# Layer 2 of a two-layer block: where the merge logits and retention gates are projected

## The chip, the cores and the metric

The kernel runs on one core of one Trainium2 chip. Its time is device microseconds of one execution, from the first to the last instruction; lower is better. All arithmetic is 32-bit: the matmuls take float32 values split into two fp32r parts (a rounded one and the rest), three products for each.

## The reference, cut to what matters

The program computes two transformer-like layers for 1,024 tokens of width 1,024. The change lies in the second layer alone:

```python
h = rms_norm(x, norm_gain[layer])
proj = jnp.einsum('bsd,dc->bsc', h, w_in[layer])          # 10 x 1024 columns
(sb_q, sb_k, sb_v, sb_g, r_q, r_k, r_v, r_g, m_sb, m_ret) = jnp.split(proj, SPLIT_POINTS, axis=-1)
...
out_a = merge_heads(stick_breaking_attention(qa, ka, va)) * jax.nn.silu(sb_g)   # 8 heads of 128
...
out_b = merge_heads(ret) * jax.nn.silu(r_g)               # chunkwise retention, 4 heads of 256
p_a = jnp.einsum('bsw,wd->bsd', out_a, w_branch_sb[layer])
p_b = jnp.einsum('bsw,wd->bsd', out_b, w_branch_ret[layer])
merged = (jax.nn.sigmoid(m_sb + b_merge[layer, 0]) * p_a
          + jax.nn.sigmoid(m_ret + b_merge[layer, 1]) * p_b)
x = x + jnp.einsum('bsd,de->bse', merged, w_out[layer])
```

The merge logits are `m_sb` and `m_ret` (columns 8192 to 10239 of the projection, 16 blocks of 128) and the retention gates are `r_g` (columns 7168 to 8191, 8 blocks of 128). Both depend only on `h`, and both are first read in the last part, where the two branches are gated and merged.

## The kernel before, in words

The normalized input of layer 2, `h2T`, stays in SBUF with the model dimension on partitions, in two parts (`h2h`, `h2l`). Every projection is a stream of matmuls over 8 slices of the model dimension and 3 products. `dense_tok` (L92) makes token-major results, 24 matmuls for each 128 tokens; `dense_col` (L107) makes a block of 128 columns for all 1,024 tokens, 48 matmuls of 512 columns into two PSUM banks; `dense_half` (L116) makes one half of such a block, 24 matmuls into one bank. These accumulators share 3 PSUM banks (tag "a").

Weights come through `load_units` (L74): for each of the 8 slices a DMA into one of 3 `raw` buffers (L64), then the split into two fp32r parts, as a rule on GpSimd (L70 a copy that rounds, L71 the difference), for the stick-breaking heads half on ScalarE and VectorE (L67, L68). The split units, `wu`, have 10 buffers of 512 columns.

Layer 2 then has these stages, in program order:

1. Eight stick-breaking heads (L970). Each has a projection of q, k and v (192 matmuls of 384 columns, L102), a per-token norm and a transposition on VectorE (L132), the head's gate (48 matmuls of 512 columns, L112), and then a chain for each of three blocks: scores (L1025), a scan on VectorE (L1039) with steps on ScalarE and GpSimd around it, transposes on TensorE (L1055), and products with v (L1060).
2. `merge_logits(0)`, 4 of the 16 blocks of merge logits, each half block evicted by ScalarE (L956) and stored by a DMA.
3. Four retention heads (L1189), each `ret_proj(h)` and then `ret_chain(h)`. `ret_proj` loads 8 units for q and k (512 columns) and projects them (192 matmuls, L112), rotates them on VectorE and GpSimd (L1100 to L1105) in place in the tiles `ro` (3 buffers for q and 3 for k, two used by a head), loads 8 units that hold v and the gate together (256 columns each), projects v (192 matmuls of 256 columns, L102), and then the gate (two blocks, 96 matmuls, L112). `ret_chain` goes through 8 chunks of 128 tokens in two groups of 4: scores of a group (L1132), transposed and decayed k (`kf`, `kd`, L1142 to L1144), and for each chunk the products L1152 and L1160, an output norm, the state's update (L1171 and VectorE) and its split (L1181, L1182). The tiles `kf` and `ob` (the transposed output) share one buffer.
4. `merge_logits(1)` to `(3)`, the other 12 blocks.
5. `gated` (L1200) loads the two branches' outputs and gates, multiplies and splits them; between and after it come the two branch projections and the output projection. Its tiles take space that the retention stage must have given back.

The order on each engine is not that of the program text: a list scheduler of the framework moves an instruction ahead when its inputs and buffers are there in the scheduler's own plan, and prefers what stands earlier in the program. On the chip the order on each engine is then fixed, and a late input holds what stands behind it. So the projection of head h+1 is already spread between the chain steps of head h.

Of the kernel before, what the change touches and what calls it, by code (L numbers as in the profile page):

```python
# [11 lines left out]
F32 = mybir.dt.float32  # L12
# [15 lines left out]
def f32(ap):  # L28
    return ap.bitcast(F32)
# [7 lines left out]
def tile_kernel(ctx: ExitStack, tc: tile.TileContext, I: dict, out: bass.AP, dbg=None, stop=None):  # L37
# [22 lines left out]
    # ---------------------------------------------------------------- helpers  # L60
# [67 lines left out]
    def dve_transpose(dst, src):  # L128
        """dst[c, x, r, t] = src[t, x, r, c], 128 by 128 for every x and r, in blocks of 32 by 32"""
        for a in range(4):  # L130
            for b in range(4):
                nc.vector.transpose(out=dst[32 * b:32 * b + 32, :, :, 32 * a:32 * a + 32],  # L132
                                    in_=src[32 * a:32 * a + 32, :, :, 32 * b:32 * b + 32])
# [54 lines left out]
    # DRAM scratch  # L188
# [14 lines left out]
    # ---------------------------------------------------------------- layer 1: norm  # L203
# [28 lines left out]
    # constants  # L232
# [7 lines left out]
    # ---------------------------------------------------------------- layer 1: dz + gates  # L240
# [25 lines left out]
    # gate scalars, [token in chunk, dir*4+head, chunk]  # L266
# [32 lines left out]
    # ---------------------------------------------------------------- layer 1: delta heads  # L299
# [4 lines left out]
    for h in range(4):  # L304
# [20 lines left out]
        # q: raw, with its norm per token  # L325
# [8 lines left out]
        # k: token major, normalized, and back  # L334
# [32 lines left out]
        for d in range(2):  # L367
# [13 lines left out]
            # decay [s, c]: with its diagonal for the products with q, strictly above it for the system  # L381
            # (the backward system is stored transposed)
# [41 lines left out]
        # operands of the scan  # L424
# [23 lines left out]
    # ---------------------------------------------------------------- layer 1: inverses of the 64-blocks  # L448
# [28 lines left out]
    # ---------------------------------------------------------------- layer 1: neighbourhood attention  # L477

    def na_proj(p, hold):
# [13 lines left out]
        for m, acc in dense_tok(hT, us, 0, 384):  # L493
            j = m % 4
            sq = na1.tile([P, 256], F32, tag="sq", name="sq", bufs=2)
            nc.scalar.activation(out=sq, in_=acc[:, 0:256], func=AF.Square)
            ss = na1.tile([P, 4], F32, tag="ss", name="ss", bufs=2)
            nc.vector.tensor_reduce(out=ss, in_=sq.rearrange("p (h d) -> p h d", h=4), op=ALU.add, axis=AX.X)
            rsqrt_small(ss, ss, 1.0 / 64, EPS, 4)
            kn = na1.tile([P, P], F32, tag="kn", name="kn", bufs=5)  # L500
            nc.scalar.copy(out=qn[:, m, :], in_=acc[:, 0:128])
            nc.scalar.copy(out=kn, in_=acc[:, 128:256])
            nc.scalar.copy(out=v[:, m, :], in_=acc[:, 256:384])
            for x, t_ in enumerate((qn[:, m, :], kn)):
                t_ = t_.rearrange("p (h d) -> p h d", h=2)
                nc.vector.tensor_tensor(out=t_, in0=t_, in1=ss[:, 2 * x:2 * x + 2].unsqueeze(2).to_broadcast([P, 2, 64]),
                                        op=ALU.mult)
            kns.append(kn)
            if j == 3:
                sl = slice((m - 3) * P, (m + 1) * P)  # L510
                # head 0 keeps its rounded part above the rest, head 1 the other way round
                pt = bank("a")
                for jj, k_ in enumerate(kns):
                    nc.tensor.transpose(pt[:, jj * P:(jj + 1) * P], k_, ident)
                for hh in range(2):
                    a, b = slice(hh * 64, hh * 64 + 64), slice(64 - hh * 64, 128 - hh * 64)
                    nc.scalar.activation(out=kS[hh][a, sl], in_=pt[a, :], func=AF.Copy, scale=gk[a])
                    nc.vector.scalar_tensor_tensor(out=kS[hh][b, sl], in0=pt[a, :], scalar=gk[a],  # L518
                                                   in1=f32(kS[hh][a, sl]), op0=ALU.mult, op1=ALU.subtract)
                kns = []  # L520
            yield 1
# [4 lines left out]
    def na_attn(p, tiles):  # L526
        qn, kS, v, z, TB = tiles[p]

        def scores(t, hh, st):
# [24 lines left out]
            if rl != ru:  # L554
                # the second row's window starts one row later: its last row takes the place of the first
                nc.tensor.matmul(ps[64:128, 0:64], lhsT=q2[:, hh, :], rhs=f32(kS[hh][:, (rl + 8) * 64:(rl + 9) * 64]),
                                 start=True, stop=True)
# [93 lines left out]
    # ---------------------------------------------------------------- layer 1: delta rule scan  # L651
# [193 lines left out]
    # ---------------------------------------------------------------- layer 1: output (transposed), layer 2: norm  # L845
    # the tokens in two sets: the inner 512, which the scan leaves first, and the outer 512
# [93 lines left out]
    # ---------------------------------------------------------------- layer 2: stick breaking attention  # L940
# [10 lines left out]
    def merge_logits(q):  # L951
        us = load_units(I["w_in_2"], 8192 + 512 * q, 512)
        for b in range(4):
            for half, acc in enumerate(dense_col(h2T, us, b * P)):
                lg = mp.tile([P, 512], F32, tag="lg", name="lg", bufs=2)
                nc.scalar.activation(out=lg, in_=acc, func=AF.Identity, bias=bm[:, 4 * q + b:4 * q + b + 1])  # L956
                nc.sync.dma_start(out=d_sg[4 * q + b, :, half * 512:half * 512 + 512], in_=lg)
# [7 lines left out]
    with tc.tile_pool(name="sb", bufs=1) as sb, tc.tile_pool(name="sr", bufs=1, side="right") as sr:  # L965
# [4 lines left out]
        for h in range(8):  # L970
# [43 lines left out]
            for ib in (0,1):  # L1014
                po = bank("o")
                ini = sb.tile([P, 4], F32, tag="ini", name="ini", bufs=2)
                for diag in ((True, False) if ib else (True,)):
                    c0 = ib * 512 if diag else 0
                    As = []
                    for i4 in range(4):  # L1020
# [28 lines left out]
                        As.append(A)  # L1049
                    for kb in range(4):  # L1050
# [14 lines left out]
                nc.sync.dma_start(out=d_oa[h, :, ib * 512:ib * 512 + 512], in_=ov)  # L1065
    if "oa" in dbg:
        nc.sync.dma_start(out=dbg["oa"], in_=d_oa)
# [3 lines left out]
    merge_logits(0)  # L1071

    # ---------------------------------------------------------------- layer 2: retention
    d_ob = dram.tile([8, P, T], F32, name="d_ob")
    d_gb = dram.tile([8, P, T], F32, name="d_gb")
    with tc.tile_pool(name="rt", bufs=1) as rt:
# [11 lines left out]
        def ret_proj(h):  # L1088
# [18 lines left out]
            us = load_units(I["w_in_2"], 6144 + 256 * h, 256, parts=2, stride=1024)  # L1107
# [7 lines left out]
            for b in range(2):  # L1115
                for half, acc in enumerate(dense_col(h2T, us, 256 + b * P)):
                    gv = mp.tile([P, 512], F32, tag="lg", name="gv", bufs=2)
                    nc.scalar.copy(out=gv, in_=acc)
                    nc.sync.dma_start(out=d_gb[2 * h + b, :, half * 512:half * 512 + 512], in_=gv)
            return rot[0], rot[1], vs  # L1120

        def ret_chain(h, tiles):
            qTs, kTs, vs = tiles
            state = None
            for g in range(2):
                qT, kT, v = qTs[g], kTs[g], vs[g]
                # scores^T of four chunks
# [19 lines left out]
                for j in range(4):  # L1147
# [6 lines left out]
                    if n > 0:  # L1154
# [3 lines left out]
                        for b in range(2):  # L1158
                            for x, (a, c) in enumerate(PASSES):
                                nc.tensor.matmul(po[:, :256], lhsT=qs[a][:, b, :], rhs=ss_[c][:, b, :], start=False,  # L1160
                                                 stop=(b == 1 and x == 2))
                    ss = rt.tile([P, 1], F32, tag="ss", name="ss", bufs=2)
# [28 lines left out]
    for q in range(1, 4):  # L1191
        merge_logits(q)
# [3 lines left out]
    # ---------------------------------------------------------------- layer 2: branches and merge  # L1196
# [135 lines left out]
```

## Time and profile before

| | |
|---|---|
| median of 3 runs | 2333.45 us (2331.77 to 2336.94) |
| the profiled execution's own time (span) | 2331.9 us |
| TensorE matmul busy | 2182.4 us (94%), 12,069 matmuls |
| VectorE busy | 1414.8 us (61%) |
| GpSimd busy | 1252.0 us (54%) |
| ScalarE busy | 863.7 us (37%) |
| mean granted TensorE clock | 0.98 |

Times of the trace count from the start of the span. The stick-breaking heads take about 830 to 1450 us, the retention heads 1450 to 1980 us, and the gating and the branch and output projections the rest. A matmul's busy time in the profile reaches from its issue to a modelled end, and consecutive matmuls overlap, so the busy share overstates how full TensorE is; the distance between consecutive matmuls in an undisturbed stream is the better measure of what one costs.

### The profile page before, as it was taken

The page shows a single profiled execution, that of the slowest core. Times are in us where ns is not written, and L with a number is a line of the kernel's source. Part 1 is how long each engine was busy: PE and PEld are TensorE (multiplying, and loading weights), DVE is VectorE, ACT ScalarE, POOL GpSimd, SP SyncE. Part 2 cuts the span into 40 slices and gives each one's busy share as a digit, 9 for nine tenths or more (in the row PEclk, how much of TensorE's full clock was granted, in tenths as well). Part 3 has the DMA queues.
Part 4 walks back from the last instruction along what each step waited for, and adds up shares of the span by engine and source line. Part 5 has one row for each costly group of instructions (what it writes and reads, how often), then busy time and mean ns, then how long its engine had stood idle before and what let it go on. Part 6 is the DMA issues. An engine that isn't in the chain of part 4 may idle for free.

```text
span 2331.9 us, 33715 instructions
## 1 busy us (share of the span) xinstructions
PE 2182.4 (94%) x12069; PEld 1864.4 (80%) x12069; DVE 1414.8 (61%) x2596; ACT 863.7 (37%) x2126; POOL 1252.0 (54%) x1467
## 2 busy tenths in 40 slices
PE   7998888999999999899889999999999999989999
PEld 7776877787888798787788777788888888767887
DVE  4688789844456568887877784426474744343221
ACT  5344334445554235554555544112222222332210
POOL 6667778851004256565565664536363633666531
PEclk9999999999999999999999999999999999999999
DMA  4266820154475421111011112211111122666433
GB/s 131 80 170 166 203 80 26 37 165 132 154 279 205 153 84 46 50 55 55 10 50 50 55 50 72 72 56 46 64 46 64 46 82 91 226 213 211 140 109 108
DMA packets 236488, 240.86 MB, mean 103 GB/s; under 512 B 39776, under 2 KB 173600, under 8 KB 236064
## 3 DMA queue, kind: packets, MB, share of 16 engines
q1 hardware_dynamic: 236320, 238.71, 32.5%
q8 instruction: 95, 1.56, 0.3%
q14 instruction: 73, 0.60, 0.1%
HBM read 167.31 MB, written 71.34 MB: 102 GB/s over the span
## 4 chain that ended last, share of the span: by engine, by line
PE 33%; DVE 16%; POOL 7%; issue 4%; DMA 4%; ACT 4%; SPq 0%; POOLq 0%; ACTq 0%; DVEq 0%
PE acc L112 21%; PE acc L102 5%; DVE qf L132 4%; PE acc L859 3%; DVE A L1039 3%; POOL A L1044 2%; DMA raw<-in_w_in_dram 1%; POOL wu L71 1%; DVE A L1035 1%; POOL ss L126 1%; DMA oa<-d_oa 1%; DVE ob L132 1%; DVE sq L988 1%; DVE wT L1058 1%; PE pt L1160 1%
## 5 line engine op out<-in xcount | busy, mean ns | idle before, releaser
L112 PE MATMUL acc<-h2h,wu 128*128 128x512 f32 x1504 | 459.1, 396 | 6.7 <-DVE sq L988 2.7
L102 PE MATMUL acc<-wu,h2h 128*128 128x384 f32 (+1 forms) x1536 | 376.2, 327 | 13.4 <-DVE sq L988 4.2
L71 POOL TENSOR_TENSOR wu<-raw,wu 128x512 fp32r<-128x512 f32 (+3 forms) x268 | 363.4, 1365 | 6.3
L70 POOL TENSOR_SCALAR wu<-raw 128x512 fp32r<-128x512 f32 (+3 forms) x268 | 205.9, 772 | 250.7 <-PE acc L112 176.7
L112 PEld LDWEIGHTS acc<-h2h,wu 128*128 128x128 f32 x1504 | 281.5, 188 | 71.9 <-ACT lg L956 3.1
L102 PEld LDWEIGHTS acc<-wu,h2h 128*128 128x128 f32 x1536 | 272.2, 194 | 21.5 <-issue 3.5
L112 PE MATMUL acc<-h2l,wu 128*128 128x512 f32 x752 | 276.1, 396 | 0.0
L102 PE MATMUL acc<-wu,h2l 128*128 128x384 f32 (+1 forms) x768 | 250.1, 327 | 0.0
L102 PE MATMUL acc<-wu,h1hi 128*128 128x384 f32 (+2 forms) x768 | 193.1, 335 | 12.6 <-DVE kS L518 6.7
L112 PE MATMUL acc<-h1hi,wu 128*128 128x512 f32 x512 | 164.3, 409 | 8.0 <-ACT pad L315 4.7
L112 PEld LDWEIGHTS acc<-h2l,wu 128*128 128x128 f32 x752 | 141.4, 188 | 31.0
L102 PEld LDWEIGHTS acc<-wu,h1hi 128*128 128x128 f32 x768 | 138.5, 196 | 17.0 <-issue 8.0
L1044 POOL TENSOR_TENSOR A<-Z,A 128x128 f32<-128x128 f32 (+2 forms) x96 | 112.4, 1176 | 70.5 <-DVE A L1039 43.6
L102 PEld LDWEIGHTS acc<-wu,h2l 128*128 128x128 f32 x768 | 148.4, 193 | 1.0
L102 PE MATMUL acc<-wu,h1lo 128*128 128x384 f32 (+2 forms) x384 | 127.8, 335 | 0.0
L112 PEld LDWEIGHTS acc<-h1hi,wu 128*128 128x128 f32 x512 | 98.1, 193 | 33.0 <-ACT pad L315 6.2
L126 POOL TENSOR_TENSOR ss<-ss,mhalf 128x2 f32<-128x2 f32 (+2 forms) x136 | 115.6, 851 | 7.2
L132 DVE STREAM_TRANSPOSE qf<-sq 32x256 f32<-32x256 f32 x256 | 111.6, 436 | 4.0
L125 POOL TENSOR_SCALAR ss<-ss 128x2 f32<-128x2 f32 (+2 forms) x136 | 42.5, 312 | 117.7 <-ACT sq L982 47.0
L1060 PE MATMUL po<-wT,v 128*128 128x512 f32 (+3 forms) x288 | 76.1, 365 | 22.2 <-DVE wT L1058 12.2
L112 PE MATMUL acc<-h1lo,wu 128*128 128x512 f32 x256 | 96.4, 405 | 0.0
L112 PE MATMUL acc<-oah,wu 128*128 128x512 f32 x256 | 81.3, 413 | 10.0 <-DVE sg L1232 6.1
(547 smaller groups left out, 4770.5 us busy)
## 6 DMA issues: line engine op xcount, KB each, us to landing
raw<-in_w_in_dram SPq DMA_DIRECT2D x192, 256.0 KB, 2.8
d_pk<-sct SPq DMA_DIRECT2D x24, 512.0 KB, 4.3
raw<-in_w_out_dram SPq DMA_DIRECT2D x40, 256.0 KB, 2.8
wsa<-d_pk SPq DMA_DIRECT2D x16, 512.0 KB, 6.0
wsb<-d_pk SPq DMA_DIRECT2D x16, 512.0 KB, 7.1
d_sg<-lg SPq DMA_DIRECT2D x32, 256.0 KB, 2.6
sg<-d_sg SPq DMA_DIRECT2D x32, 256.0 KB, 4.3
raw<-in_w_in_dram SPq DMA_DIRECT2D x32, 192.0 KB, 2.7
```

What stands on the lines that cost most here:

```text
L70: nc.gpsimd.tensor_scalar(out=u[:, 0, :], in0=raw, scalar1=1.0, scalar2=0.0, op0=ALU.mult, op1=ALU.add)
L71: nc.gpsimd.tensor_tensor(out=u[:, 1, :], in0=raw, in1=f32(u[:, 0, :]), op=ALU.subtract)
L102: nc.tensor.matmul(acc[:, :n], lhsT=hT[a][:, k, m * P:(m + 1) * P], rhs=us[k][:, b, c0:c0 + n], start=(k == 0 and i == 0), stop=(k == NK - ...
L112: nc.tensor.matmul(accs[half], lhsT=us[k][:, b, c0:c0 + P], rhs=hT[a][:, k, half * 512:(half + 1) * 512], start=(k == 0 and i == 0), stop= ...
L125: nc.gpsimd.tensor_scalar(out=dst, in0=src, scalar1=mul, scalar2=eps, op0=ALU.mult, op1=ALU.add)
L126: nc.gpsimd.tensor_tensor(out=dst, in0=dst, in1=mhalf[:, :eshape], op=ALU.pow)
L132: nc.vector.transpose(out=dst[32 * b:32 * b + 32, :, :, 32 * a:32 * a + 32], in_=src[32 * a:32 * a + 32, :, :, 32 * b:32 * b + 32])
L859: nc.tensor.matmul(acc, lhsT=us[k][:, y, (b % 4) * P:(b % 4 + 1) * P], rhs=token_set(mT[x][:, k, 0:T], s), start=(k == 0 and i == 0), stop ...
L988: nc.vector.scalar_tensor_tensor(out=sq[:, a * P:(a + 1) * P], in0=acc[:, a * P:(a + 1) * P], scalar=ss[:, a:a + 1], in1=gqk[:, a, :], op0 ...
L1039: nc.vector.tensor_tensor_scan(out=A[:, :w][:, ::-1], data0=A[:, :w][:, ::-1], data1=A[:, :w][:, ::-1], initial=0.0 if diag else ini[:, i4 ...
L1044: nc.gpsimd.tensor_tensor(out=A[:, :w], in0=Z[:, :w], in1=A[:, :w], op=ALU.subtract)
L1060: nc.tensor.matmul(po[:, i0 * P:512], lhsT=v[a][:, c0 // P + kb, :], rhs=wT[b][:, :n], start=(diag and kb == 0 and x == 0), stop=(diag == ...
```

## The change

The function `merge_logits` and its calls are gone. In its place a generator, `filler`, goes through 24 blocks of 128 columns, the 16 of the merge logits first and then the 8 of the retention gates. For each block it loads two units of 4 slices each into buffers of its own (`fu`, 3 of them, beside the 10 of `wu`; `raw` and the accumulators are shared as before), splits them on GpSimd, and gives the two halves one after the other with `dense_half`, each with its eviction and its store. The program takes half blocks from it in these places: one in each of the three blocks of every stick-breaking head, between the scan steps and the transposes (24), five after the last of these heads, and one in each of the 8 chunks of the last retention head's chain, between the output's products and its norm. What is left (11) follows that chain. `ret_proj` loads and projects v alone, without the gate.

```diff
-    def merge_logits(q):
-        us = load_units(I["w_in_2"], 8192 + 512 * q, 512)
-        for b in range(4):
-            for half, acc in enumerate(dense_col(h2T, us, b * P)):
+    d_gb = dram.tile([8, P, T], F32, name="d_gb")
+    fp = ctx.enter_context(tc.tile_pool(name="fp", bufs=1))
+
+    def filler(blocks):
+        for b in blocks:
+            cols = slice(8192 + b * P, 8192 + (b + 1) * P) if b < 16 else slice(7168 + (b - 16) * P, 7168 + (b - 15) * P)
+            us = []
+            for g in range(2):
+                raw = wraw.tile([P, 4, P], F32, tag="raw", name="raw", bufs=3)
+                nc.sync.dma_start(out=raw, in_=I["w_in_2"][g * 512:(g + 1) * 512, cols].rearrange("(k p) c -> p k c", p=P))
+                u = fp.tile([P, 2, 4, P], F32R, tag="fu", name="fu", bufs=3)
+                nc.gpsimd.tensor_scalar(out=u[:, 0], in0=raw, scalar1=1.0, scalar2=0.0, op0=ALU.mult, op1=ALU.add)
+                nc.gpsimd.tensor_tensor(out=u[:, 1], in0=raw, in1=f32(u[:, 0]), op=ALU.subtract)
+                us += [u[:, :, k, :] for k in range(4)]
+            for half in range(2):
+                hs = slice(half * 512, half * 512 + 512)
+                acc = dense_half(h2T, us, 0, half)
                 lg = mp.tile([P, 512], F32, tag="lg", name="lg", bufs=2)
...
+                if b < 16:
+                    nc.scalar.activation(out=lg, in_=acc, func=AF.Identity, bias=bm[:, b:b + 1])
+                    nc.sync.dma_start(out=d_sg[b, :, hs], in_=lg)
+                else:
+                    nc.scalar.copy(out=lg, in_=acc)
+                    nc.sync.dma_start(out=d_gb[b - 16, :, hs], in_=lg)
+                yield 1
+
+    fill = filler(range(24))
...
                         last_sb = nc.scalar.activation(out=A[:, :w], in_=A[:, :w], func=AF.Exp)
                         As.append(A)
+                    take(fill, 1)
                     for kb in range(4):
...
+        take(fill, 5)
...
-    merge_logits(0)
...
-            us = load_units(I["w_in_2"], 6144 + 256 * h, 256, parts=2, stride=1024)
+            us = load_units(I["w_in_2"], 6144 + 256 * h, 256)
...
-            for b in range(2):
-                for half, acc in enumerate(dense_col(h2T, us, 256 + b * P)):
-                    gv = mp.tile([P, 512], F32, tag="lg", name="gv", bufs=2)
-                    nc.scalar.copy(out=gv, in_=acc)
-                    nc.sync.dma_start(out=d_gb[2 * h + b, :, half * 512:half * 512 + 512], in_=gv)
...
+                    if h == 3:
+                        take(fill, 1)
                     ss = rt.tile([P, 1], F32, tag="ss", name="ss", bufs=2)
...
-    for q in range(1, 4):
-        merge_logits(q)
+    drain(fill)
```

## Rows read from the trace of the kernel before

**Rows 1.** The page, part 1: busy time of each engine over the span.

```profile
PE 2182.4 (94%) x12069; PEld 1864.4 (80%) x12069; DVE 1414.8 (61%) x2596; ACT 863.7 (37%) x2126; POOL 1252.0 (54%) x1467
```

**Rows 2.** Busy time by stretch: window, its length, busy us (and count) by engine.

```profile
1002.00:1374.00 372.00, 333.16 (x1758) 293.38 (x1757) 298.52 (x580) 189.07 (x561) 219.59 (x286) 0.99 0.14 43
1374.00:1450.00 76.00, 74.74 (x358) 60.96 (x357) 46.30 (x77) 34.98 (x80) 43.35 (x55) 1.00 0.20 67
1865.00:1980.00 115.00, 115.00 (x559) 95.75 (x558) 55.30 (x103) 27.72 (x56) 45.25 (x54) 1.00 0.26 85
1980.00:2120.00 140.00, 125.00 (x511) 96.35 (x510) 61.13 (x65) 48.24 (x78) 93.53 (x76) 0.98 0.67 221
```

**Rows 3.** The chain of waits in order of time: start us, us, engine and line.

```profile
854.31 16.62 PE acc L102 x93
...
1451.11 23.25 PE acc L112 x100
...
1622.79 6.65 PE acc L102 x56
```

**Rows 4.** TensorE's waits, 1076 to 1374 us: total us, times, longest.

```profile
PE po L1060 <- DVE wT L1058: 7.6, 10, 1.8
PE po L1060 <- ACT wT L1057: 4.5, 4, 2.3
```

**Rows 5.** Instructions on tile `raw`, 1000 to 1460 us: count, ns min/median/max.

```profile
L64 SPq DMA_DIRECT2D raw<-in_w_in_dram x55: 327/374/642, 1013.3 to 1459.7; - x55
L70 POOL TENSOR_SCALAR wu<-raw x36: 614/624/1066, 1011.3 to 1457.0; 128x512 fp32r<-128x512 f32 x36
L71 POOL TENSOR_TENSOR wu<-raw,wu x36: 1265/1292/1731, 1012.0 to 1457.7; 128x512 fp32r<-128x512 f32 x36
...
L68 DVE TENSOR_TENSOR wu<-raw,wu x19: 691/1249/1772, 1019.0 to 1317.5; 128x512 fp32r<-128x512 f32 x19
...
DMA to landing us min/median/max: 2.6/2.9/5.1
```

**Rows 6.** Line 956, whole span: the eviction of one half block of merge logits.

```profile
L956 ACT ACTIVATE lg<-acc,bm x32: 671/682/707, 1408.3 to 2046.7; 128x512 f32<-128x512 f32 x32
```

**Rows 7.** The chain of waits: gate projections of retention heads 0, 1 and 3.

```profile
1532.23 22.30 PE acc L112 x96
...
1642.15 22.31 PE acc L112 x96
...
1865.07 22.30 PE acc L112 x96
```

**Rows 8.** VectorE in order of time, second retention head: start us, us, instruction, [idle before].

```profile
1639.40 7.19 DVE L132 STREAM_TRANSPOSE ob<-ot 32x256 f32<-32x256 f32 x16
...
1650.20 7.18 DVE L132 STREAM_TRANSPOSE kf<-ro 32x256 f32<-32x256 f32 x16 [3.15 <-DMA d_ob<-ob]
1658.60 1.28 DVE L1144 SCALAR_TENSOR_TENSOR kd<-kf,rdv,kd 128x1024 fp32r<-128x1024 f32 x1 [1.22 <-ACT kd L1143]
```

**Rows 9.** TensorE in order of time, the same head's chain.

```profile
1637.81 1.50 PE L1132 MATMUL pz<-ro 128*128 128x128 f32 x12
...
1664.31 0.60 PE L1132 MATMUL pz<-ro 128*128 128x128 f32 x4
...
1678.34 0.52 PE L1152 MATMUL pt<-v,wT 128*128 128x256 f32 x3
...
1686.62 0.51 PE L1152 MATMUL pt<-v,wT 128*128 128x256 f32 x3
```

**Rows 10.** ScalarE in order of time: evictions of the next head's q.

```profile
1681.25 0.59 ACT L1095 COPY ro<-acc 128x512 f32<-128x512 f32 x1 [0.32 <-PE acc L112]
...
1694.16 1.08 ACT L1095 COPY ro<-acc 128x512 f32<-128x512 f32 x2 [4.47 <-PE acc L112]
```

**Rows 11.** Line 112 alone by stretch: matmul busy (count), weight loads busy (count).

```profile
1865.00:1980.00 115.00, 102.37 (x430) 79.81 (x430) 1.00 0.26 85
```

**Rows 12.** Line 1207: the loads of the first branch's gates in `gated`.

```profile
L1207 SPq DMA_DIRECT2D ga<-d_ga x16: 319/320/645, 1981.5 to 2048.6; - x16
```

More of the change, by code (lines that the diff above doesn't have):

```diff
@@ L949, in tile_kernel @@
     nc.sync.dma_start(out=bm, in_=I["b_merge_2"])
-    def merge_logits(q):
-        us = load_units(I["w_in_2"], 8192 + 512 * q, 512)
-        for b in range(4):
-            for half, acc in enumerate(dense_col(h2T, us, b * P)):
-                lg = mp.tile([P, 512], F32, tag="lg", name="lg", bufs=2)
-                nc.scalar.activation(out=lg, in_=acc, func=AF.Identity, bias=bm[:, 4 * q + b:4 * q + b + 1])
-                nc.sync.dma_start(out=d_sg[4 * q + b, :, half * 512:half * 512 + 512], in_=lg)
+    d_gb = dram.tile([8, P, T], F32, name="d_gb")
[14 more added lines that the diff above has]
+                acc = dense_half(h2T, us, 0, half)
+                lg = mp.tile([P, 512], F32, tag="lg", name="lg", bufs=2)
+                if b < 16:
[6 more added lines that the diff above has]
+    fill = filler(range(24))
     d_oa = dram.tile([8, P, T], F32, name="d_oa")
@@ L1069, in tile_kernel @@
         return
-    merge_logits(0)
     d_ob = dram.tile([8, P, T], F32, name="d_ob")
-    d_gb = dram.tile([8, P, T], F32, name="d_gb")
     with tc.tile_pool(name="rt", bufs=1) as rt:
@@ L1319 @@
     from concourse.bass_utils import run_bass_kernel_spmd as _run
-    nc = _bacc.Bacc("TRN2", target_bir_lowering=False, num_devices=1)
+    nc = _bacc.Bacc("TRN2", target_bir_lowering=False, num_devices=1, dynamic_dma_scratch_size=1024)
     host = host_arrays(inputs)
```

## The prediction, made before the changed kernel was run

> **What bounds the kernel now.** I read the page first. TensorE is busy 94% of the span and no other engine comes near it [rows 1], so the first thought is that work moved about on a full engine gains nothing. The second view, stretches of time, shows why that thought is too short: the count of matmuls in a stretch, each at the distance that it has in an undisturbed stream, is less than the stretch. The distances come from solid runs in the chain of waits: 100 matmuls of 512 columns in 23.25 us, so 0.2325 us; 93 of 384 columns in 16.62 us, 0.179 us; 56 of 256 columns in 6.65 us, 0.119 us [rows 3]; 12 of 128 columns in 1.50 us, 0.12 us [rows 9]. A stick-breaking head has 192 of 384 columns (34.3 us), a gate of 48 (11.2 us), 72 for scores and products with v, 27 widths of 512 in all (12.6 us for the two together: 2 x 27 x 0.2325), and 36 transposes (4.3 us): 62.4 us and 348 matmuls. Five heads, 1002 to 1374 us, hold 1758 matmuls in 372 us [rows 2]: 74.4 us a head, of which 62.4 x 1758/1740 = 63 is work and **11.4 us a head is idle**. The third view, who waited for whom, says what for: above all for the steps of the chain, VectorE's and ScalarE's halves of wT [rows 4]. VectorE is busy 298.5 of the 372 us, 80%, in order, so its lateness is passed on.
>
> The same sum for the other stages. Retention: the gate projections of head 0 and head 3 start 332.8 us apart, so a head takes 110.9 us [rows 7]; its work is 192 + 96 matmuls of 512 columns (67.0), 192 of 256 (22.8), and 140 in the chain at about 0.12 (16.8), 106.6 us: 4.3 us idle. Gating, 1980 to 2120 us: 511 matmuls at 0.2325 are 118.8 of 140 us, 21 us idle [rows 2].
>
> TensorE's work doesn't change, so the sum goes by idle time alone, stage by stage, against the profiled execution's 2331.9 us.
>
> **The change, part by part.** *The half blocks themselves.* `dense_half` has the 24 matmuls that half of `dense_col` has, each with its own weight load in both, so 24 x 0.2325 = 5.6 us and no change in total. One bank in place of two changes nothing that I can see. Cost 0.
>
> *Three half blocks in each stick-breaking head.* 16.7 us of TensorE work that waits for no chain step, only for two loads (landing after a median of 2.9 us) and two splits (0.62 + 1.29 us each on GpSimd) [rows 5], in buffers of its own. A head would then need 63 + 16.7 = 79.7 us of TensorE against 74.4 us now. If every idle moment took filler, the head would take 79.7 us and 11.4 us would be hidden; if none did, 91.1 us. Before, merge_logits(0) was spread along the last head's chain, and there 358 matmuls fill the 76 us with TensorE 98% busy by the profile's measure, against 90% in the five heads [rows 2]. That stretch shows that ready work does fill the gaps, but it lacks the next head's norms. I take 83.7 us, nearer the filled stretch: 74.4 + 16.7 - 83.7 = 7.4 us hidden in each of heads 0 to 6, **52 us**. The last head had 8 half blocks along its chain and has 3 + 5 now: 0. Bounds: 0 and 7 x 11.4 = 80 us.
>
> What else these issue: per head 3 splits, 5.7 us on GpSimd, busy 59% there; 3 evictions of 0.68 us on ScalarE [rows 6], 51% busy; 3 loads and 3 stores, each some 0.37 us on SyncE's queue [rows 5], where stores wait for their eviction and the next head's loads stand behind them. A load that comes 1 or 2 us later is covered, since the head's units are loaded a head ahead. Without that cover the price is the landing, 2.9 us a head. I price them at nothing beyond the 83.7 us.
>
> GpSimd's splits touch VectorE. The same VectorE subtraction of 128x512 took from 0.69 to 1.77 us in one stretch [rows 5]. The Trainium skill (SBUF — State Buffer, section SBUF: two separate sides) calls the pair of ports between VectorE and GpSimd an exclusive lock, held for a whole instruction, against a VectorE operation with two SBUF inputs; the spread agrees. By that rule the 5.7 us of splits could each hold VectorE once, 59.7 + 5.7 = 65.4 us a head; scaled with its waits (74.4/59.7) a head would be paced by VectorE at 81.5 us, under my 83.7, so 9.6 a head would be hidden and the sum would be 2331.9 - 67 + 18 + 13 + 1.5 = 2297; that lies in the forecast's own range, and it gets no chance of its own.
>
> *The retention gates leave heads 0 to 2.* TensorE loses 22.3 us of work a head, which is conserved; but this work is cover. The scheduler put the gate, earlier in the program, ahead of the chain: 12 of the first group's 16 scores came before it, from 1637.8, and the last 4 only at 1664.3, as it ended [rows 7, 9]. Without it the chain may go on from v's end, 1642. The decayed k is not ready before 1659.9 (transposes at 1650.2 behind the store of the previous output, then 7.2 + 1.3 us and ScalarE between) [rows 8], 18 us after v. What can TensorE do in that time? Project the next head's q and k. But `ro` has three buffers, so half 1 of the next q can't be evicted before the first group of this chain is done with its q: half 0 was evicted at 1681.25, half 1 not before 1694.16 [rows 10]. With three accumulators only two column blocks (22.3 us) can run ahead, plus some 7 us of chain, plus units that come late as v's buffers are released: about 34 us after v. The buffer comes free after 18 us and three chunk steps. A step now takes 8.3 us (1678.34 to 1686.62) [rows 9], which is 43 us: 9 us short. If steps shrink to about half, 31 us, nothing is short. I take 6 us a head, **18 us** for heads 0 to 2, from 0 to 36 (12 a head, if units come late as well).
>
> The v units are half as wide: about 1 us of GpSimd less for each of 8, off the transition to v. This hides in the same idle time; a gain of at most 4.3 us a head, 13 in all, is the bound on that side.
>
> *The last head and the tail.* From 1865 to 1980, 430 matmuls of line 112 ran [rows 11], 18 half blocks of the 28 (4 gate, 24 merge) there were: 10, some 56 us, remained to cover `gated`, whose loads for the first branch run from 1981.5 to 2048.6, 67 us [rows 12]. Now 19 half blocks are left at v's end. Without the gate ahead of it the chain takes 115 - 22 = 93 us, 17 of its own work and 76 for 13 or 14 half blocks; 5, some 30 us, remain. With the first branch block (11 us) that covers 41 of 67 us. Now 21 us is idle in all; up to 26 more would be, and fewer units compete for GpSimd and SyncE's queue, so I take half: **13 us**, from 0 to 27.
>
> *Sum.* 2331.9 - 52 + 18 + 13 = 2311 us. The execution's own time lies 1.5 us under the median of the runs (2333.45), so 2312.
>
> **The rivals.** *Hidden and kept.* TensorE is full in all stick-breaking heads (-70) and the retention chain steps shrink, so nothing is lost there, with 10 lost in the tail: 2331.9 - 70 + 10 + 1.5 = 2273. For it: the filled stretch. Against it: VectorE at 80%, with lateness that order alone doesn't cure.
>
> *A wash.* 33 us is hidden and 31 given back as cover that is missing later: 2331.9 - 2 + 1.5 = 2331. For it: the cover was used in full, no idle time from 1865 to 1980 [rows 2].
>
> *Slower.* The half blocks run as a lump at the start of each chain, ahead of the next head's projection, because they stand earlier in the program; VectorE, which paces the head, then gets that projection's results later and its waits return behind the lump. Then a head takes 74.4 us and most of 16.7 more. It decides when a head takes over 86.7 us (less than 31 us hidden in seven heads). At 90 us, 8 us is hidden: 2331.9 - 8 + 31 + 1.5 = 2356.
>
> **How the numbers follow.** 0.5 for the forecast, its own range 2290 to 2328; 0.14 for hidden and kept; 0.12 for the wash; 0.24 for slower. 0.2% is 4.7 us, about what a measurement of this kernel can tell from no change. Faster has the forecast and the first rival, 0.64; the wash lies within, 0.12; slower has 0.24. The range for 8 in 10 leaves off the far parts of both sides: 2275 to 2346.
>
> **What would show it.** In the changed profile, the gates of consecutive stick-breaking heads (L112) some 84 us apart (right), over 87 (the rival); the time between matmuls there down to 3 to 5 us a head, with the waits for wT shrunk. In retention, head to head 95 us with TensorE waiting for ScalarE's or GpSimd's `ro`; 84 to 88 would mean no lost cover, and over 100 that I priced it too low. In the tail, the chain ending near 1980 again and a longer stretch with fewer than 86 matmuls in 20 us. The prediction is wrong if the chip's stick-breaking heads don't take the filler into their waits, or if the retention chain, rid of the gate, is either much shorter than 93 us or holds TensorE far longer.

## The result, and the profile after

The change made the kernel 0.8% slower. Timed in turn with the kernel before, the changed kernel takes 2353.01 us (median of 4, 2349.69 to 2354.88) against 2334.98; the ratio is 1.0082, 95% interval 1.0067 to 1.0097. The forecast was 2312. Its profiled execution takes 2351.4 us, 19.5 more than that of before.

The page's first part shows the same work on each engine as in [rows 1]: the 12,069 matmuls, and GpSimd's few more and shorter instructions.

```profile
PE 2184.7 (93%) x12069; PEld 1860.5 (79%) x12069; DVE 1414.4 (60%) x2596; ACT 864.5 (37%) x2126; POOL 1246.1 (53%) x1499
```

So the 19.5 us are idle time of TensorE, and its place is found by setting the stages' lengths against their work. Four marks of each trace do it: the last product of the stick-breaking heads, the last v product of the retention heads, the first load of `gated`, and the end. The line's matmuls, with the first and the last start, of before and then of after:

```profile
L1060 PE MATMUL po<-wT,v x288: 220/392/628, 912.9 to 1450.7; 128*128 128x512 f32 x80, 128*128 128x256 f32 x32, 128*128 128x384 f32 x16, 128*128 128x128 f32 x16
```

```profile
L1083 PE MATMUL po<-wT,v x288: 220/390/502, 917.3 to 1551.9; 128*128 128x512 f32 x80, 128*128 128x256 f32 x32, 128*128 128x384 f32 x16, 128*128 128x128 f32 x16
```

After, v's last product (line 102, from 1500 to 1950 us) and the loads of the first branch's gates (which answer to [rows 12]):

```profile
L102 PE MATMUL acc<-wu,h2h x512: 274/282/582, 1596.3 to 1905.4; 128*128 128x256 f32 x171
```

```profile
L1224 SPq DMA_DIRECT2D ga<-d_ga x16: 319/319/432, 2014.5 to 2076.1; - x16
```

And the half blocks (line 120) in the last chain and from the gating's start on: busy time and count of matmuls, then of weight loads.

```profile
1905.00:2014.00 109.00, 98.37 (x411) 75.96 (x412) 1.00 0.29 98
```

```profile
2014.00:2154.00 140.00, 10.86 (x47) 8.43 (x45) 0.84 0.64 212
```

| stage | before, us | after, us | longer by | work added (matmuls x 0.2325) | idle time more |
|---|---|---|---|---|---|
| to the end of the stick-breaking heads | 1450.7 | 1551.9 | 101.2 | 21 half blocks, 117.2 | **-16** |
| to v of the last retention head | 414.1 | 353.5 | -60.6 | 12 gate halves gone, -67.0 | **+6** |
| to the gating's start | 116.7 | 109.1 | -7.6 | 413 in place of 437, -5.6 | **-2** |
| to the end | 350.4 | 336.9 | -13.5 | 43 in place of 235, -44.6 | **+31** |

(Before, 8 half blocks stood in the first of these stages; after, 24 + 5. The counts of the last two are those of the merge and gate matmuls between the marks themselves, [rows 11] on before's side. Other work crosses the marks too, up to 19 matmuls in a stage, so an entry of the last column is good to some 2 us.) The last column sums to the 19.5 us. The heads hid 16 of the 52 us that were forecast, and the tail lost 31 where 13 was forecast.

Two stretches show both, after: five head periods, and 140 us from the gating's start. They answer to the first and last of [rows 2].

```profile
1046.00:1480.00 434.00, 406.38 (x2104) 355.86 (x2102) 304.23 (x571) 195.00 (x564) 234.51 (x306) 1.00 0.17 53
...
2014.00:2154.00 140.00, 106.25 (x370) 75.93 (x369) 59.90 (x72) 47.77 (x78) 74.85 (x61) 0.84 0.64 212
```

A head takes 434/5 = 86.8 us; its work is 62.4 + 16.7 us, with the count 2104 for 2100 79.3, so 7.5 us is idle, against 11.4. That is 20 us in five heads; what lies before and behind them gave 4 back. In the tail 370 matmuls at 0.2325 are 86 of 140 us: 54 us idle (or, in part, at a lower clock, as the last section shows), against 21 to 22 (140 us from 1982 held 507). What TensorE waited for there:

```profile
PE acc L112 <- ACT oah L1231: 21.6, 12, 6.0
PE acc L112 <- DVE sg L1249: 6.4, 2, 4.7
PE acc L112 <- DVE oal L1232: 3.7, 7, 1.2
PE acc L112 <- POOL wu L71: 2.0, 2, 1.3
```

`oah` and `oal` are the gated operands of the first branch. Before, TensorE had merge logits to project while they were made, and the two cost 1.7 us of waiting in 140 us.

### The profile page after: what moved, and what is told of

It reads as the page before. It is cut to its first block, busy times and chain, and to the rows that moved or that the text cites. A ratio compares the mean times of both kernels' runs of the same rounds, so it can differ in the third digit from the quotient of the medians.

```text
span 2351.4 us, 33826 instructions
## 1 busy us (share of the span) xinstructions
PE 2184.7 (93%) x12069; PEld 1860.5 (79%) x12069; DVE 1414.4 (60%) x2596; ACT 864.5 (37%) x2126; POOL 1246.1 (53%) x1499
## 4 chain that ended last, share of the span: by engine, by line
PE 33%; DVE 15%; POOL 8%; DMA 5%; ACT 4%; issue 4%; SPq 0%; POOLq 0%; ACTq 0%; DVEq 0%
PE acc L112 15%; PE acc L102 6%; PE acc L120 4%; DVE qf L132 4%; PE acc L859 3%; DVE A L1061 3%; DMA raw<-in_w_in_dram 2%; POOL A L1066 2%; DVE A L1057 1%; POOL ss L126 1%; PE po L1083 1%; DVE A L1052 1%; POOL wu L71 1%; DMA oa<-d_oa 1%; ACT A L1053 1%
## 5 line engine op out<-in xcount | busy, mean ns | idle before, releaser
L71 POOL TENSOR_TENSOR wu<-raw,wu 128x512 fp32r<-128x512 f32 (+3 forms) x236 | 300.7, 1283 | 5.7
L70 POOL TENSOR_SCALAR wu<-raw 128x512 fp32r<-128x512 f32 (+3 forms) x236 | 167.2, 713 | 170.9 <-PE acc L112 83.9
L120 PE MATMUL acc<-h2h,fu 128*128 128x512 f32 x768 | 251.4, 399 | 0.0
L112 PE MATMUL acc<-h2h,wu 128*128 128x512 f32 x736 | 227.9, 395 | 0.0
L120 PEld LDWEIGHTS acc<-h2h,fu 128*128 128x128 f32 x768 | 143.5, 189 | 31.1
L112 PEld LDWEIGHTS acc<-h2h,wu 128*128 128x128 f32 x736 | 137.7, 188 | 30.4
L1066 POOL TENSOR_TENSOR A<-Z,A 128x128 f32<-128x128 f32 (+2 forms) x96 | 117.8, 1234 | 80.0 <-DVE A L1061 43.7
L120 PE MATMUL acc<-h2l,fu 128*128 128x512 f32 x384 | 152.2, 396 | 0.0
L112 PE MATMUL acc<-h2l,wu 128*128 128x512 f32 x368 | 136.8, 395 | 0.0
L112 PE MATMUL acc<-oah,wu 128*128 128x512 f32 x256 | 92.2, 442 | 30.0 <-ACT oah L1231 21.6
```

What stands on the lines that cost most here:

```text
L70: nc.gpsimd.tensor_scalar(out=u[:, 0, :], in0=raw, scalar1=1.0, scalar2=0.0, op0=ALU.mult, op1=ALU.add)
L71: nc.gpsimd.tensor_tensor(out=u[:, 1, :], in0=raw, in1=f32(u[:, 0, :]), op=ALU.subtract)
L112: nc.tensor.matmul(accs[half], lhsT=us[k][:, b, c0:c0 + P], rhs=hT[a][:, k, half * 512:(half + 1) * 512], start=(k == 0 and i == 0), stop= ...
L120: nc.tensor.matmul(acc, lhsT=us[k][:, b, c0:c0 + P], rhs=hT[a][:, k, half * 512:(half + 1) * 512], start=(k == 0 and i == 0), stop=(k == N ...
L1066: nc.gpsimd.tensor_tensor(out=A[:, :w], in0=Z[:, :w], in1=A[:, :w], op=ALU.subtract)
```

## The experiments

Each kernel is timed in turn with the kernel before; the ratio is to that. Idle time is worked out as above, from lengths and counts of matmuls.

**Chain first.** The eight half blocks leave the last chain and stand behind it.

```diff
-                    if h == 3:
-                        take(fill, 1)
```

> The changed kernel without the eight half blocks inside the last retention chain: they follow the chain in the program, 19 in all. Theory 1 (the tail lost its cover: the half blocks stood ahead of the chain's steps and were used up when the gating began): the chain ends earlier, 5 to 9 half blocks are left when the gating's loads begin, idle time of TensorE from there on falls by 15 to 30 us, time 2322 to 2338 us. Rival (the gating itself got slower, whatever stands beside it): idle time stays, 2348 to 2356 us.

Measured 2352.57 us, 1.0079 (1.0054 to 1.0105): the same as the change, and the 140 us from the gating's start hold 375 matmuls (53 us idle).

```profile
2014.00:2154.00 140.00, 107.05 (x375) 77.00 (x374) 59.48 (x72) 47.76 (x78) 75.48 (x61) 0.84 0.66 215
```

The scheduler had put the half blocks between the chain's steps either way: 17 of them, as in the change. So their place in the program, ahead of the chain's steps, which I had taken for the reason that they were used up, is no part of the cause.

**None in the heads.** Eight half blocks stand behind the heads, the other 40 behind the last chain.

```diff
-                    take(fill, 1)
...
-        take(fill, 5)
+        take(fill, 8)
...
-                    if h == 3:
-                        take(fill, 1)
```

> No half blocks in the stick-breaking heads and none inside the last retention chain; 8 after the heads (as many merge blocks as stood there before), the other 40 after the chain. Retention gates stay out of the retention heads. Theory 1: the tail has more cover than it needs (idle there 25 us or less, as before), the heads are as before (74 us each), the retention heads keep the 10 us more idle that the changed kernel has: 2336 to 2348 us. Rival (the retention heads are what made it slower, and the filled heads hid that): over 2352 us.

Measured 2355.31 us, 1.0084 (1.0065 to 1.0102). The time is what the rival said, the reason isn't: from the heads' end (1455) to the last v (1813) it loses 6 us, just as the change does. With 23 half blocks left at the gating's start, the first 140 us hold 544 matmuls, 13.5 us idle; but the tail as a whole is 80 us longer than before for 72 us more work (544 for 235 matmuls), and the heads end 5 us later.

```profile
1923.00:2063.00 140.00, 131.85 (x544) 104.25 (x543) 39.36 (x34) 36.31 (x60) 83.00 (x76) 0.96 0.55 175
```

So too much left for the tail costs as well; that the second branch waits for the input's space is argued from the code alone.

**In the projection.** The three half blocks of a head go into its loop over tokens.

```diff
             for n_, (m, acc) in enumerate(dense_tok(h2T, us, 0, 384, order=order)):
+                if n_ in (1, 3, 5):
+                    take(fill, 1)
...
-                    take(fill, 1)
```

> The three half blocks of each stick-breaking head stand inside its projection loop (after tokens 1, 3 and 5) and not in its chain; the rest is as in the changed kernel. Theory 2 (in the changed kernel the three run as one lump of 17 us behind the head's gate, where no projection can run, and hide little): heads some 82 us apart and not 86, 20 to 30 us less idle in the heads, 2320 to 2335 us. Rival (GpSimd's splits for the half blocks, or the chain's own engines, set the heads' pace): heads stay 85 to 88 us apart, 2346 to 2356 us.

Measured 2380.08 us, 1.0191 (1.0170 to 1.0212), far off. Heads are 442/5 = 88.4 us apart, worse than 86.8, though the half blocks lie apart there, and the first scores start at 919.5 and not at 889.6 us: 92 matmuls of half blocks stand ahead of them, and not 46. So spreading them over the projection doesn't help, and the theory of the lump falls in that form; another way to spread them wasn't tried.

```profile
1077.00:1519.00 442.00, 416.48 (x2130) 365.65 (x2129) 315.96 (x580) 199.41 (x568) 251.01 (x313) 0.98 0.17 55
```

**The form alone.** The half blocks with their loads and buffers, but in the places of before, and the gates back in the retention heads.

```diff
-    fill = filler(range(24))
+    fill = filler(range(16))
...
-                    take(fill, 1)
...
-        take(fill, 5)
+        take(fill, 8)
...
-            us = load_units(I["w_in_2"], 6144 + 256 * h, 256)
+            us = load_units(I["w_in_2"], 6144 + 256 * h, 256, parts=2, stride=1024)
...
+            for b in range(2):
+                for half, acc in enumerate(dense_col(h2T, us, 256 + b * P)):
```

> Merge logits in 128-column half blocks with the new function, loads and buffers, but where they stood before: 8 half blocks after the stick-breaking heads, 24 after the retention heads; retention gates as before in each retention head. Theory (the form costs nothing, the places do): 2328 to 2340 us. Rival (one accumulator bank, loads of 512-byte rows or the buffers cost time): over 2343 us.

Measured 2340.11 us, 1.0017 (1.0002 to 1.0031). The form of the merge logits costs some 4 us (0.5 to 7 by the interval).

**Extra work in the tail.** The last gate block is projected three more times.

```diff
-    fill = filler(range(24))
+    fill = filler(list(range(24)) + [23] * 3)
```

> The changed kernel plus six half blocks of repeated work behind the others (the last gate block projected three times more, 6 x 24 matmuls, 33 us of TensorE): the output is the same. Theory 1 (from the start of the gating TensorE waits for loads and splits with nothing to do): the added work lies in that idle time, the kernel takes 0 to 10 us longer than the changed one, 2351 to 2363 us. Rival (TensorE's own stream sets the end in this stretch too): 33 us longer, 2382 to 2390 us.

Measured 2361.27 us, 1.0101 (1.0084 to 1.0117): 8 us over the change by the medians, 4 by the two ratios, for 33.5 us of added work. Line 120 has 197 matmuls from the gating's start on in place of 47, and the 140 us are full but for 26 us:

```profile
2018.00:2158.00 140.00, 124.20 (x489) 95.05 (x488) 64.13 (x68) 47.76 (x79) 93.57 (x78) 0.93 0.71 230
```

Three quarters of the added work or more cost nothing: TensorE had nothing to do there.

**Two in a head** (not in the third block of a chain), and **one in a head** (in the first block, with 8 behind the heads).

```diff
-                    take(fill, 1)
+                    if diag:
+                        take(fill, 1)
```

```diff
-                    take(fill, 1)
+                    if ib == 0:
+                        take(fill, 1)
...
-        take(fill, 5)
+        take(fill, 8)
```

> Two half blocks in each stick-breaking head in place of three (not in the third block), so that 8 more follow later: 27 half blocks from the last retention head's v on, as many as there were before (28). Theory 1 (a half block hides 0.8 us in the heads and covers 3 to 4 us in the tail): 9 to 11 half blocks left when the gating starts, idle time there back from 56 to 25 to 30 us, heads 5 to 8 us more idle, 2322 to 2338 us. Rival (the tail's idle time isn't a matter of how many are left): no change in the tail, 2348 to 2358 us.

> One half block in each stick-breaking head, eight behind them, 32 from the last retention head's v on. Theory 1: 13 to 15 are left when the gating starts, so the first branch is covered in full, but the second branch's operands reuse the input's space and can't be written before the last half block has run: idle 25 to 32 us in the tail; the heads 12 us more idle than in the changed kernel: 2330 to 2345 us. Rival (the places in the heads set the time): heads' idle falls in proportion to the half blocks, and the time lies within 3 us of the changed kernel.

Two: 2323.77 us, **0.9953** (0.9936 to 0.9970), faster than before. One: 2338.19 us, 0.9999 (0.9985 to 1.0013). Windows of the two kernels: four head periods, and 140 us from the gating's start.

```profile
1126.00:1444.00 318.00, 302.91 (x1588) 265.96 (x1587) 244.12 (x456) 153.72 (x448) 191.75 (x240) 1.00 0.17 53
1972.00:2112.00 140.00, 126.52 (x515) 98.43 (x513) 62.99 (x64) 48.22 (x80) 96.46 (x80) 0.96 0.70 222
```

```profile
1103.00:1409.00 306.00, 285.99 (x1493) 253.09 (x1493) 232.09 (x455) 149.56 (x442) 175.94 (x230) 0.98 0.15 48
```

With two, the tail is back at 140 - 515 x 0.2325 = 20 us idle, and a head takes 79.5 us for 73.8 of work (1588 matmuls for 1584): 5.7 us idle, less than with three. With one it is 8.3. That a third half block adds idle time was in no theory.

**One load.** The change with the half blocks' weights loaded and split once and used for all blocks.

```diff
-            us = []
-            for g in range(2):
+            if b == 0:
+                us = []
+            for g in range(2 if b == 0 else 0):
```

> The changed kernel with the half blocks' weights loaded and split once, for the first block, and used for all 24: the other 46 loads and 46 pairs of GpSimd splits are left out, and the merge logits and gates hold that block's values. Theory 3 (GpSimd's splits hold VectorE and the chain, so that the heads hide little): heads 81 to 83 us apart and not 86, idle in the heads 20 to 35 us less, 2315 to 2332 us. Rival (the order on TensorE is fixed by a plan in which the chain's engines are faster than on the chip, so the waits for the chain stay whatever GpSimd does): heads 84 to 87 us apart, 2343 to 2354 us.

**Loads without splits.** The same, but with every load kept.

```diff
-            us = []
+            if b == 0:
+                us = []
             for g in range(2):
                 raw = wraw.tile([P, 4, P], F32, tag="raw", name="raw", bufs=3)
...
+                if b:
+                    continue
```

> As the kernel that loads and splits the half blocks' weights once, but with all 48 loads kept and only the splits after the first block left out; the merge logits and gates hold the first block's values. Theory 3 (GpSimd's splits, 5.7 us a head, are what the third half block costs): heads 83 to 85 us apart as with one load, idle in the heads 45 to 52 us, 2317 to 2327 us. Rival (the loads, in SyncE's queue and the three raw buffers that the heads' own loads share): heads 86 to 87 us apart, idle 65 to 75 us, 2340 to 2352 us.

One load: 2319.41 us, 0.9921 (0.9906 to 0.9936). Loads without splits: 2338.61 us, 1.0000 (0.9989 to 1.0011). Five head periods of each:

```profile
1043.00:1460.00 417.00, 401.57 (x2100) 355.66 (x2099) 304.66 (x569) 195.07 (x564) 211.12 (x282) 1.00 0.15 48
```

```profile
1051.00:1464.00 413.00, 399.81 (x2104) 355.94 (x2102) 295.43 (x570) 195.75 (x564) 211.17 (x282) 1.00 0.19 61
```

83.4 and 82.6 us a head against 86.8: without the splits a head idles 3 to 4 us in place of 7.5, loads or not. The whole time of the second is 12 us over what theory 3 said; the excess lies behind the heads, where it needs 799 us to the end, as the change does, and one load 787. The two kernels differ in the loads alone, so they are the price there; which of the work behind the heads they delay was not tried. VectorE's busy time in five heads is 304.7 and 295.4 us in these two and 304.2 with the splits, so it tells little of them.

**Four in a head**, and **two in other places** (second and third block).

```diff
-                    take(fill, 1)
+                    take(fill, 1 if diag else 2)
```

```diff
-                    take(fill, 1)
+                    if ib:
+                        take(fill, 1)
```

> Four half blocks, two whole blocks, in each stick-breaking head in place of three (32, 5 behind the heads, 8 in the last chain, 3 left). Theory 4 (an odd number of halves makes heads with one block's loads and splits and heads with two alternate, and the plan fits neither): 4 to 5 us idle a head as with two, heads 63 + 22.3 + 4.5 = 90 us apart. Rival (each further load and split delays the chain by itself): 8 us idle or more, heads over 93 us. In both the tail has no cover: 50 us or more idle there, 2345 to 2375 us.

> Two half blocks in each stick-breaking head as in the kernel with two, but in the second and third block of the chain and not in the first and second. If the number decides and not the place: heads 78 to 80 us apart, 2320 to 2332 us. If the place decides: heads 81 us or more apart, 2335 to 2350 us.

Four: 2388.72 us, 1.0215 (1.0197 to 1.0232); 468/5 = 93.6 us a head for 84.7 of work, 8.8 idle.

```profile
1056.00:1524.00 468.00, 436.19 (x2222) 382.22 (x2221) 306.60 (x570) 199.47 (x569) 239.76 (x318) 0.99 0.18 56
```

An even number doesn't help, so theory 4 falls: each further block delays the chain. (Heads with the splits of one block and of two do alternate in the change; what they cost is read from that further below.) The other two: 2334.19 us, 0.9975 (0.9963 to 0.9986); 409/5 = 81.8 us a head, 7.3 idle against 5.7. So place counts beside number in the heads, by one profile of each; the intervals of the two ratios overlap.

**Splits elsewhere**: on ScalarE and VectorE, with three in a head as in the change, and with two in heads 1 to 7; and the latter with its splits on GpSimd, **two from head 1**.

```diff
-                nc.gpsimd.tensor_scalar(out=u[:, 0], in0=raw, scalar1=1.0, scalar2=0.0, op0=ALU.mult, op1=ALU.add)
-                nc.gpsimd.tensor_tensor(out=u[:, 1], in0=raw, in1=f32(u[:, 0]), op=ALU.subtract)
+                nc.scalar.copy(out=u[:, 0], in_=raw)
+                nc.vector.tensor_tensor(out=u[:, 1], in0=raw, in1=f32(u[:, 0]), op=ALU.subtract)
```

```diff
-                    take(fill, 1)
+                    if diag and h:
+                        take(fill, 1)
```

> The changed kernel with the half blocks' splits on ScalarE (rounding) and VectorE (difference) and none on GpSimd. If GpSimd's queue is what the splits cost: heads 82 to 84.5 us apart, idle in the heads 45 to 55 us, 2320 to 2335 us. If the split work costs wherever it stands (VectorE is at 70% of a head): heads 86 to 90 us apart, 2348 to 2365 us.

> The kernel with two half blocks in heads 1 to 7, with the splits on ScalarE and VectorE. If GpSimd's queue is what counts: heads 77 to 78.5 us apart and not 79, 2314 to 2324 us. If the split work costs wherever it stands: heads 79 us or more, 2322 to 2335 us.

> The kernel with two half blocks in a head, but none in head 0 (14 in the heads, 29 from the last retention head's v on). In the kernel with two, the time before the first scores held 10 us more idle time than before the change and the second head took 93 us in place of 79. If the half blocks of head 0 are the cause (they compete with the first head's own start): 10 to 20 us less idle, 2308 to 2318 us. If not: 2322 to 2332 us.

Splits elsewhere, three a head: 2353.54 us, 1.0073 (1.0051 to 1.0095), heads 429/5 = 85.8 us apart.

```profile
1049.00:1478.00 429.00, 405.30 (x2101) 354.16 (x2100) 304.07 (x584) 201.62 (x578) 201.69 (x278) 1.00 0.17 54
```

Two a head: 2325.56 us, 0.9951 (0.9936 to 0.9966), heads 80.0 us apart. So GpSimd's queue is not what the splits cost; they cost nearly as much on the other pair of engines. Two from head 1, splits on GpSimd: 2325.45 us, **0.9938** (0.9913 to 0.9962), heads 396/5 = 79.2 us apart, and the tail full but for 21 us.

```profile
1028.00:1424.00 396.00, 377.21 (x1976) 331.40 (x1976) 302.35 (x568) 192.79 (x559) 239.96 (x300) 1.00 0.17 53
1956.00:2096.00 140.00, 125.23 (x511) 98.54 (x510) 61.35 (x64) 47.86 (x79) 90.27 (x75) 0.96 0.69 218
```

It can't be told from two in every head by time. Its profile, 2326.2 us, is 2 us shorter than that one's, not 10 to 20: the second head takes 84 us in place of 93, but two half blocks more lie in the tail.

## Why the prediction was wrong

*Half blocks cost what they did.* Right to within some 4 us: 12,069 matmuls, and the form alone 1.0017.

*52 us hidden in the heads.* Wrong by 36 of the 40 us that the sum missed; the tail adds 18, the retention heads gave 12 back and the stretch before the gating 2. Two steps failed. The first is "I price them at nothing beyond the 83.7 us", said of splits, evictions, loads and stores. Without the splits a head takes 82.6 to 83.4 us, the size that I had taken; with them 86.8. The stage ends at 1533.8 us with one load, at 1537.4 with loads and no splits, and at 1551.9 in the change: 15 to 18 of the 36 us.

The trace of the change shows this price by itself. A block's two splits serve two half blocks, so with three half blocks in a head, heads with four splits and heads with two alternate. Two neighbours, first all engines, then the splits on GpSimd:

```profile
1132.00:1220.90 88.90, 81.73 (x422) 70.72 (x421) 61.15 (x115) 39.12 (x113) 49.85 (x64) 1.00 0.18 57
1220.90:1306.40 85.50, 80.48 (x421) 70.85 (x420) 61.62 (x115) 39.07 (x113) 46.42 (x60) 1.00 0.17 53
```

```profile
1132.00:1220.90 88.90, 9.22 (x8) 1.00 0.18 57
1220.90:1306.40 85.50, 4.84 (x4) 1.00 0.17 53
```

The same 420 matmuls (one that crosses a mark counts on both sides) take 3.4 us longer with two splits more; the next pair is 89.1 and 84.4 us. With loads and no splits these heads take 82.2 and 81.6 us, with the splits on ScalarE and VectorE 87.0 and 84.8. So a split costs some 1 to 2 us of a head. By what way isn't shown. It is felt at the chain's steps: TensorE waited longer for ScalarE's eviction of the scores (`Z`) and VectorE's half of `wT`, and less for `ini`. Five heads of the change, then of loads without splits:

```profile
PE pz L1047 <- ACT Z L1050: 9.7, 9, 1.8
PE po L1083 <- DVE wT L1081: 7.5, 10, 1.5
...
PE po L1083 <- DVE ini L1065: 2.0, 2, 1.0
```

```profile
PE po L1086 <- DVE ini L1068: 6.7, 4, 1.7
PE pz L1050 <- ACT Z L1053: 4.3, 4, 2.1
PE po L1086 <- DVE wT L1084: 1.0, 1, 1.0
```

The second step that failed is "hidden in each of heads 0 to 6". The five heads of [rows 2] hid 20 us, and 36 to 40 without the splits, but the rest of the stage gave 4 back (1 to 10 without the splits), where I had counted 15 for the other two heads. Why the rest of the stage hides nothing stays open.

With zero to four half blocks a head, the idle time is 11.4, 8.3, 5.7, 7.5 and 8.8 us: work without inputs from the chain fills gaps until its own preparation makes new ones. I had read the last head, where 8 half blocks stood, as showing what the gaps take; that head has no norms of a next head beside it, as I said, and it was the wrong one to lean on.

The lock between GpSimd and VectorE (the Trainium skill, SBUF — State Buffer, section SBUF: two separate sides) would have left 9.6 us hidden a head; 4.3 was measured (91.1 - 86.8). VectorE's busy time shows no sign of it inside the trace: 61.2 us in the head with four splits above, 61.6 in the one with two. Between kernels it varies by up to 10 us in five heads (304.2 with the splits on GpSimd, 304.7 and 295.4 with none, and 294.2 with them moved, their own 9.9 us left out), so a price of up to 2 us a head isn't excluded.

*18 us lost in the retention heads.* Right in sign, too large: 6. The failed step is "I take 6 us a head". From v's end to v's end, three head periods of the change:

```profile
1627.90:1713.10 85.20, 82.69 (x510) 73.29 (x509) 54.21 (x92) 20.70 (x51) 53.18 (x64) 1.00 0.14 44
1713.10:1803.80 90.70, 88.28 (x556) 78.90 (x555) 65.10 (x110) 25.14 (x57) 47.48 (x59) 1.00 0.14 45
1803.80:1905.50 101.70, 89.44 (x526) 78.77 (x525) 64.80 (x120) 23.00 (x54) 48.29 (x61) 0.95 0.13 39
```

By the same sum as in the prediction the first two hold 82.6 and 88.1 us of work, so 2.6 us is idle in each, less than the 4.3 of before; the loss is all in the third, 17 us idle. The largest wait of the stage, new and 9.0 of its 9.4 us in the third period, is until VectorE has emptied the bank of a chunk's output (`ot`), not for `ro`:

```profile
PE pt L1168 <- DVE ot L1183: 9.4, 4, 3.8
PE acc L102 <- DVE v L1135: 3.6, 3, 2.0
...
PE pz L1148 <- POOL ro L1125: 1.7, 1, 1.7
```

So the mechanism that I described, TensorE blocked by the q buffers, can't be seen. What sets the third period apart stays open.

*13 us in the tail.* Right in mechanism, too small: 31. The failed step is "17 of its own work and 76 for 13 or 14 half blocks": 17 of the 19 half blocks went between v's end and the gating, and TensorE was full for 109 us there, where I had 93. The chain's own length was near to that. With four half blocks a head only 11 were left to stand beside it, and the stretch still took 98 us, 24 of them idle:

```profile
1955.60:2053.90 98.30, 78.12 (x375) 64.03 (x373) 52.23 (x103) 22.76 (x49) 50.33 (x60) 0.89 0.29 97
```

So the scheduler put more ahead of the gating than the chain's waits hold, 2 half blocks were left in place of 5, and "fewer units compete for GpSimd and SyncE's queue, so I take half" had nothing to stand on. The extra work shows the cause, and 8 half blocks moved back from the heads undo it.

*The rivals.* The one that said slower had its deciding point at 86.7 us a head, and 86.8 was measured; but the agreement is luck. The half blocks of a head do stand close together (1139 to 1162 us in one head), yet spread over the projection they cost more, and the price follows the splits. And the time came out over before because of the tail: without its 31 us it would lie 12 under.

## What to carry to other kernels

Moving ready work into the gaps of a stage is no gain by itself when TensorE's total is fixed: ask what the work covered where it stood, and count how many pieces are left there. Here a half block hid under 1 us in the heads and was worth 3 to 4 us in the tail. Price the preparation of a filler (loads, splits, evictions) against the chain that it is to hide in, and try the number: two of three half blocks a head gave 0.9953, three 1.0082.

## What the runs showed of the hardware

When TensorE ran out of work in the tail, its clock fell: the same stage, 50 us of after and 50 us of before, from 20 and 28 us behind the gating's start (the column behind the counts is the granted clock).

```profile
2034.00:2084.00 50.00, 29.47 (x61) 16.04 (x61) 22.05 (x29) 16.83 (x27) 21.13 (x16) 0.64 0.45 148
```

```profile
2010.00:2060.00 50.00, 45.11 (x189) 34.74 (x188) 20.50 (x22) 18.30 (x30) 31.73 (x26) 1.00 0.59 195
```

0.64 is a mean over both levels, 1.2 and 2.4 GHz. TensorE in order of time shows the lower one: after a wait of 6 us for `oah` the matmuls of 512 columns stood 0.43 us apart (2036.67 to 2037.10 to 2037.52) and not 0.2325:

```profile
2035.06 1.22 PE L112 MATMUL acc<-oah,wu 128*128 128x512 f32 x2 [5.99 <-ACT oah L1231]
...
2036.67 0.63 PE L112 MATMUL acc<-oah,wu 128*128 128x512 f32 x1
2037.10 0.63 PE L112 MATMUL acc<-oal,wu 128*128 128x512 f32 x1
2037.52 1.05 PE L112 MATMUL acc<-oah,wu 128*128 128x512 f32 x2
```

Of the 54 us idle in the 140 us window, the waits listed above are 33.7. Of the other 20, 8 are 42 matmuls that stood 0.43 us apart with no wait between them; the rest lies beside the waits, where a matmul's own distance can't be read. The kernels with the most idle time in this window show the lowest clocks, 0.77 with four half blocks a head (340 matmuls) to 0.97 before (507). So TensorE paid twice for its waits here, and my price for lost cover left the second part out.
